# A hybrid decoder trunk: the places of the pooled parts on their way to DRAM, and the temporaries of the input sums

## The chip, the core and the metric

The kernel runs on one core of a Trainium2 chip. The core has five engines with instruction streams of their own: TensorE (PE) multiplies matrices out of SBUF into PSUM; VectorE (DVE) and ScalarE (ACT) do elementwise work; GpSimd (POOL) and SyncE (SP) here only issue transfers (DMAs). An engine takes its instructions in order and waits at one whose semaphores are not there yet. The metric is the device time in microseconds (us) of one execution; the median of three runs counts.

## The reference

One layer with two residual steps on x (512 tokens, 1024 channels, fp32). Cut to what matters:

```python
h = _rms(x, norm1_w) * (1 + sc1) + sh1
z, xbc, dt_raw, q, k, v, u, gates = split(h @ w_in)
y_ssd  = ssd(xbc, dt_raw, z) @ w_ssd_out
y_attn = dilated_attention(q, k, v) @ w_attn_out
y_pool = (_multi_scale_pool(u, w_pool_mix) * pool_scale) @ w_pool_out
g_ssd, g_attn, g_pool = split(sigmoid(gates))
x = x + g1 * ((g_ssd * y_ssd + g_attn * y_attn + g_pool * y_pool) @ w_out)
h = _rms(x, norm2_w) * (1 + sc2) + sh2
x = x + g2 * (square(relu(h @ w_ff1)) @ w_ff2)
```

The pooling takes the 1024 channels of u in four groups of 256. Each group gets the mean over its window (2, 4, 8 or 16 tokens) less u itself, and then a 256 x 256 matrix of its own:

```python
outs.append((csg - shifted) / count - ug[:, :, gi])      # group gi
pooled = stack(outs);  einsum('bsgi,gio->bsgo', pooled, w_pool_mix)
```

## The kernel before

**Tiles.** Activations lie with channels on the 128 partitions and 512 tokens along them, in SBUF tiles of 128 x 512. Such tiles live in 49 equal places. `blk(name)` takes the place that has been idle longest, `free` puts a place at the end of the list of idle ones; who takes a place waits until everything that read or wrote it has finished, a transfer to DRAM included. The eight PSUM banks are handed out by the same rule.

**Products.** Each fp32 product is made of three matmuls (`mm3`, L305 to L307): both factors are split into a high part (the value rounded to fp32r) and a low part (the rest), and high x low, high x high and low x high are added in PSUM. A weight pair (128 x 1024) is loaded by SP into `raw`, cast by ScalarE into `wh`, and its low part `wl` is made by VectorE (L288), or, in the stretch of this change (`st["adds"]`, `wsplit_add`), by ScalarE writing the negative of `wh` (L281) and POOL issuing an accumulating transfer of the weight onto it (L282).

**The stretch of the change.** After the attention's projection come, on TensorE, the products for u (`pool`), the gate of the SSD branch, `gate(GS, 0)`, with the four groups of the pooling's mixing put between its weight pairs, and the product with w_ssd_out, `project(a["w_ssd_out"], 8, 0, ...)`, whose first matmul in the profile is `psacc<-ynl,wh`. `project` needs four PSUM banks; two of them are those that the last mixing group leaves.

`pool_mix(gi)` does one mixing group: for each half m (128 channels) six matmuls into a bank `psmix`, then ScalarE writes the high part x, scaled, into SBUF (L1164), VectorE the low part y (L1165), the bank is freed, and POOL issues the transfers of both to DRAM (L1169). They are brought back much later as `poolh` and `pooll`. The SBUF places of x and y are the list `stage`: four of them, taken at the first group and used by all four groups, x and y of half m in `stage[2 * m : 2 * m + 2]`, so that each group writes where the group ahead of it is still being sent from. They are freed after the last group.

`input_sums(xh, xl)` makes sums of the eight input tiles that `seven_products` needs (a product of two-by-two blocks with seven block products instead of eight; its matmuls are L823). Four pieces, k = 0 to 3; each adds high and low part of tiles k and k + 4 into t1 and t2 (L765, L766: full width, 128 x 512), forms x and y in four half-width steps (L767 to L770), and splits x and y into `txh`, `txl`, `tyh`, `tyl` (a ScalarE cast L332 and a VectorE subtraction L333 each). Each piece takes four places for t1, t2, x and y and frees them at its end. It is used twice: during the gate and w_ssd_out's product (the pieces are spread between weight pairs, `side.extend(sums)`), for all gates after it, and in the MLP (all four pieces at once, ahead of `second(0)`).

**What sets the order.** The code is traced in the order it is written; pieces of side work are traced by `tick()` after each weight pair. A scheduler then sets the order of each engine's instructions by its own estimates of when operands and places are there, with preference for what stands in `tc.high_priority`. So another place for a tile, and with it another set of waits, also gives another order. `seven_products` sums its weights on VectorE with high priority (`wsum` and `rawl`, L805 to L808, from `rawl` and `raw` loaded by SP, L789 and L790); those of the gate that follows are made in this stretch already.

Of the kernel before, what the change touches and what calls it, by code (L numbers as in the profile page):

```python
# [11 lines left out]
F32R = mybir.dt.float32r  # L12
# [86 lines left out]
def kernel(ctx: ExitStack, tc: tile.TileContext, a: dict, out: bass.AP, dbg=None):  # L99
# [35 lines left out]
    def blk(name, dt=F32):  # L135
        return sb.take(name, dt)
# [620 lines left out]

    def input_sums(xh, xl):

        tq = []  # L760

        def piece(k):
            def go():
                t1, t2, x, y = (blk("tq") for _ in range(4))
                V.tensor_tensor(t1, xh[k].bitcast(F32), xl[k].bitcast(F32), ALU.add)  # L765
                V.tensor_tensor(t2, xh[k + 4].bitcast(F32), xl[k + 4].bitcast(F32), ALU.add)  # L766
                V.tensor_tensor(x[:, ta], t1[:, tb], t1[:, ta], ALU.subtract)  # L767
                V.tensor_tensor(x[:, tb], t2[:, tb], x[:, ta], ALU.subtract)
                V.tensor_tensor(y[:, ta], t2[:, tb], t1[:, tb], ALU.subtract)
                V.tensor_tensor(y[:, tb], t2[:, ta], x[:, tb], ALU.subtract)  # L770
                tq.append((split(x, "tx"), split(y, "ty")))
                free(t1, t2, x, y)

            return go

        return tq, [piece(k) for k in range(4)]
# [376 lines left out]
    def pool_mix(gi):  # L1153
        wh, wl = mixw[gi]
        if gi == 0:

            stage.extend(blk("pool", F32R) for _ in range(4))
        for m in range(2):
            ps = psm("mix")
            cs = slice(m * P, (m + 1) * P)  # L1160
            for k in range(2):
                mm3(ps, wh[:, k, cs], wl[:, k, cs], dh[2 * gi + k], dl[2 * gi + k], k == 0, k == 1)
            x, y = stage[2 * m : 2 * m + 2]
            S.activation(x, ps, AF.Copy, scale=vc("pool_scale", gi * 2 + m))  # L1164
            V.scalar_tensor_tensor(y, ps, vc("pool_scale", gi * 2 + m), x.bitcast(F32), ALU.mult, ALU.subtract)  # L1165
            free(ps)
            for t, l in ((x, ph_), (y, pl_)):
                l.append(dp.tile([P, T], F32, name=uid("pool")))
                nc.gpsimd.dma_start(l[-1], t.bitcast(F32))  # L1169
        if gi == 3:  # L1170
            free(*stage)
        free(*dh[2 * gi : 2 * gi + 2], *dl[2 * gi : 2 * gi + 2])
# [375 lines left out]
```

## Time and profile before

| | |
|---|---|
| median of 3 runs | 1096.71 us (1096.25 to 1097.31) |
| profiled execution | 1095.79 us, its span 1094.0 us |
| granted TensorE clock, mean | 0.998 |
| busy: TensorE, VectorE, ScalarE, POOL | 1083.0, 748.4, 548.2, 39.9 us |

A timeline row gives the start in the span, the duration, engine, line, operation, output and inputs, and in brackets how long the engine had been idle and what ended that. Starts one after another on an engine are closer than the durations, since instructions overlap. "DMA to landing" is the time from the issue of a transfer to its end. Names in the profile are without numbers: `pool<-psmix,vec` is a high part of the pooling, `pool<-psmix,vec,pool` a low part, `tq` are the sums' temporaries, `psacc` a bank of a product.

### The profile page before, as it was taken

The page shows a single profiled execution, that of the slowest core. Times are in us where ns is not written, and L with a number is a line of the kernel's source. Part 1 is how long each engine was busy: PE and PEld are TensorE (multiplying, and loading weights), DVE is VectorE, ACT ScalarE, POOL GpSimd, SP SyncE. Part 2 cuts the span into 40 slices and gives each one's busy share as a digit, 9 for nine tenths or more (in the row PEclk, how much of TensorE's full clock was granted, in tenths as well). Part 3 has the DMA queues.
Part 4 walks back from the last instruction along what each step waited for, and adds up shares of the span by engine and source line. Part 5 has one row for each costly group of instructions (what it writes and reads, how often), then busy time and mean ns, then how long its engine had stood idle before and what let it go on. Part 6 is the DMA issues. An engine that isn't in the chain of part 4 may idle for free.

```text
span 1094.0 us, 15636 instructions
## 1 busy us (share of the span) xinstructions
PE 1083.0 (99%) x6022; PEld 935.0 (85%) x6022; DVE 748.4 (68%) x1429; ACT 548.2 (50%) x889; POOL 39.9 (4%) x70
## 2 busy tenths in 40 slices
PE   8999999999999999999989999999999999999998
PEld 7878888888887888888869889899889989989987
DVE  7955746683677966667866657567697587687664
ACT  8965874543544943756455335354344334335330
POOL 0000000000000010001311100000000000000000
PEclk9999999999999999999999999999999999999999
DMA  9823253546554343247855543460214224233032
GB/s 342 305 97 91 68 158 120 191 154 203 182 174 146 105 142 101 78 121 189 242 179 181 146 135 116 138 228 1 84 52 155 74 80 136 63 111 136 20 116 77
DMA packets 50958, 148.71 MB, mean 136 GB/s; under 512 B 6066, under 2 KB 6834, under 8 KB 50884
## 3 DMA queue, kind: packets, MB, share of 16 engines
q1 hardware_dynamic: 43088, 126.08, 34.5%
q0 software_dynamic: 7072, 20.45, 7.6%
q10 hardware_dynamic: 724, 1.18, 0.3%
q8 instruction: 47, 0.77, 0.3%
q14 instruction: 27, 0.22, 0.1%
HBM read 141.37 MB, written 6.32 MB: 135 GB/s over the span
## 4 chain that ended last, share of the span: by engine, by line
PE 95%; DVE 2%; DMA 1%; ACT 1%; issue 0%; SPq 0%; POOL 0%; DVEq 0%; ACTq 0%
PE psacc L305 22%; PE psacc L306 22%; PE psacc L307 22%; PE psacc L823 17%; PE psacc L545 4%; PE psS L624 1%; PE psy L1084 1%; DMA pool<-pool 1%; PE pso L740 1%; PE psyo L1092 1%; PE pso L738 1%; DMA xT<-in_x_dram 0%; PE psqT L603 0%; PE pskT L608 0%; PE psst L1043 0%; PE pspT L721 0%
## 5 line engine op out<-in xcount | busy, mean ns | idle before, releaser
L288 DVE TENSOR_TENSOR wl<-raw,wh 128x1024 fp32r<-128x1024 f32 x116 | 141.6, 1221 | 128.6 <-ACT wh L288 120.7
L288 ACT CAST wh<-raw 128x1024 fp32r<-128x1024 f32 x116 | 121.6, 1049 | 188.6 <-PE psacc L306 108.3
L305 PE MATMUL psacc<-hl,wh 128*128 128x512 f32 x320 | 128.8, 403 | 0.2 <-ACT pT L722 0.2
L307 PE MATMUL psacc<-hh,wl 128*128 128x512 f32 x320 | 124.7, 390 | 0.0
L306 PE MATMUL psacc<-hh,wh 128*128 128x512 f32 x320 | 124.6, 389 | 0.0
L306 PE MATMUL psacc<-ah,wh 128*128 128x512 f32 (+1 forms) x260 | 100.4, 386 | 0.0
L305 PE MATMUL psacc<-al,wh 128*128 128x512 f32 (+1 forms) x260 | 100.4, 386 | 0.0
L307 PE MATMUL psacc<-ah,wl 128*128 128x512 f32 (+1 forms) x260 | 100.3, 386 | 0.0
L305 PE MATMUL psacc<-wl,rh 128*128 128x512 f32 x192 | 77.4, 403 | 0.0
L307 PE MATMUL psacc<-wh,rl 128*128 128x512 f32 x192 | 75.2, 392 | 0.0
L306 PE MATMUL psacc<-wh,rh 128*128 128x512 f32 x192 | 75.1, 391 | 0.0
L305 PEld LDWEIGHTS psacc<-hl,wh 128*128 128x128 f32 x320 | 60.1, 188 | 13.5 <-issue 1.2
L306 PEld LDWEIGHTS psacc<-hh,wh 128*128 128x128 f32 x320 | 60.2, 188 | 13.3 <-issue 1.4
L307 PEld LDWEIGHTS psacc<-hh,wl 128*128 128x128 f32 x320 | 60.0, 188 | 12.8
L1467 DVE SCALAR_TENSOR_TENSOR xr<-psacc,modv,xr 128x512 f32<-128x512 f32 (+1 forms) x65 | 44.7, 738 | 18.7 <-PE psacc L307 18.7
L799 DVE TENSOR_TENSOR wl<-rawl,wh 128x512 fp32r<-128x512 f32 (+1 forms) x36 | 33.6, 953 | 34.5 <-ACT wh L798 34.4
L307 PEld LDWEIGHTS psacc<-ah,wl 128*128 128x128 f32 x260 | 48.8, 188 | 9.8
L305 PEld LDWEIGHTS psacc<-al,wh 128*128 128x128 f32 x260 | 48.9, 188 | 9.7
L306 PEld LDWEIGHTS psacc<-ah,wh 128*128 128x128 f32 x260 | 48.9, 188 | 9.7
L798 ACT CAST wh<-wsum 128x1024 fp32r<-128x1024 f32 x18 | 19.0, 1053 | 70.9 <-PE psacc L306 69.0
L798 ACT CAST wh<-rawl 128x512 fp32r<-128x512 f32 (+1 forms) x36 | 29.1, 833 | 48.7 <-PE psacc L306 28.3
L305 PEld LDWEIGHTS psacc<-wl,rh 128*128 128x128 f32 x192 | 36.1, 188 | 7.7 <-ACT qT L604 0.5
(426 smaller groups left out, 2781.1 us busy)
## 6 DMA issues: line engine op xcount, KB each, us to landing
raw<-in_w_in_dram SPq DMA_DIRECT2D x74, 512.0 KB, 3.6
raw<-in_w_ff_dram SPq DMA_DIRECT2D x52, 512.0 KB, 3.7
wa<-in_w_ada_dram SPq DMA_DIRECT2D x64, 256.0 KB, 3.5
wada<-in_w_ada_dram SPq DMA_DIRECT2D x14, 512.0 KB, 7.9
rawl<-in_w_ff_dram SPq DMA_DIRECT2D x12, 512.0 KB, 3.5
wst<-in_w_in_dram SPq DMA_DIRECT2D x16, 256.0 KB, 7.8
M<-prow POOLq DMA_DIRECT2D x16, 256.0 KB, 3.7
wl<-in_w_in_dram POOLq DMA_DIRECT2D x8, 512.0 KB, 5.7
```

Of the source, the lines that this page charges most:

```text
L288: edges[:] = S.copy(wh, raw), V.tensor_tensor(wl, raw, wh.bitcast(F32), ALU.subtract)
L305: mm(ps, lhsT=wh, rhs=xl, start=first, stop=False)
L306: mm(ps, lhsT=wh, rhs=xh, start=False, stop=False)
L307: mm(ps, lhsT=wl, rhs=xh, start=False, stop=last)
L545: mm(ps[j], lhsT=t[:, j, :], rhs=w, start=first, stop=last)
L624: mm(so[b], lhsT=qT[:, b * P : (b + 1) * P], rhs=kT[:, (b + 1) * P - n : (b + 1) * P], start=True, stop=True)
L738: mm(od, lhsT=vs[kb][:, hs], rhs=pT[b // 2][:, cs : cs + P], start=(b == 0), stop=False, skip_group_check=True)
L740: mm(ov[:, b, :], lhsT=vs[b][:, hs], rhs=pT[0][:, b * P : (b + 1) * P], start=False, stop=(gi == 2 and b == 3), skip_group_check=True)
L798: S.copy(h, x)
L799: V.tensor_tensor(l, x, h.bitcast(F32), ALU.subtract)
L823: mm(o, lhsT=x[:, cs], rhs=y, start=first and k == 0 and j == 0 and n == 0, stop=k == 3 and n == 2, skip_group_check=True)
L1467: V.scalar_tensor_tensor(xT[d][:, ts], p[:, : ts.stop - ts.start], modv[:, 3, d : d + 1], xT[d][:, ts], ALU.mult, ALU.add)
```

## The change

Two edits. `pool_mix` takes eight places at the first group instead of four, and groups 0 and 2 use the first four, groups 1 and 3 the other four. `input_sums` takes the four temporaries once, at the first piece, all pieces use them, and they are freed after the last.

```diff
     def input_sums(xh, xl):
-        tq = []
+        tq, tmp = [], []
         def piece(k):
             def go():
-                t1, t2, x, y = (blk("tq") for _ in range(4))
+                if k == 0:
+                    tmp.extend(blk("tq") for _ in range(4))
+                t1, t2, x, y = tmp
...
                 tq.append((split(x, "tx"), split(y, "ty")))
-                free(t1, t2, x, y)
+                if k == 3:
+                    free(*tmp)
...
         if gi == 0:
-            stage.extend(blk("pool", F32R) for _ in range(4))
+            stage.extend(blk("pool", F32R) for _ in range(8))
...
-            x, y = stage[2 * m : 2 * m + 2]
+            x, y = stage[4 * (gi % 2) + 2 * m : 4 * (gi % 2) + 2 * m + 2]
```

The number of instructions on each engine is the same. The lines behind the first edit move down by 3: L1165 is L1168 in the changed kernel, L805 is L808, and the sums L765 to L770 are L767 to L772. On POOL and SP the order is the same; on TensorE one matmul of w_ssd_out's product stands later. VectorE and ScalarE differ around the mixing groups and around the MLP's pieces. The rows that follow have the names with their numbers; the last number of a name counts all tiles.

VectorE around group 1 of the mixing (psmix_1034 and psmix_1037 before, psmix_1038 and psmix_1041 now, are the banks of its two halves; wsum is the first weight sum of the gate to come). Before:

```order
L1165 SCALAR_TENSOR_TENSOR pool_1019_4898<-psmix_1034_4965,vec_1_79,pool_1018_4897 128x512
L765 TENSOR_TENSOR tq_1080_5197<-hh1_247,hl1_255 128x512
L333 TENSOR_TENSOR pdl_1010_4859<-win_1008_4853,pdh_1009_4858 128x512
L765 TENSOR_TENSOR tq_1069_5148<-hh0_246,hl0_254 128x512
L767 TENSOR_TENSOR tq_1071_5150<-tq_1069_5148 128x256
L1165 SCALAR_TENSOR_TENSOR pool_1021_4900<-psmix_1037_4978,vec_1_79,pool_1020_4899 128x512
L805 TENSOR_TENSOR wsum_1116_5335<-rawl_1110_5321,raw_1111_5322 128x2x256
L768 TENSOR_TENSOR tq_1071_5150<-tq_1070_5149,tq_1071_5150 128x256
```

Now, in the same place (the wsum is row 687 of VectorE):

```order
L1168 SCALAR_TENSOR_TENSOR pool_1023_4902<-psmix_1038_4969,vec_1_79,pool_1022_4901 128x512
L1168 SCALAR_TENSOR_TENSOR pool_1025_4904<-psmix_1041_4982,vec_1_79,pool_1024_4903 128x512
L333 TENSOR_TENSOR pdl_1010_4859<-win_1008_4853,pdh_1009_4858 128x512
L768 TENSOR_TENSOR tq_1074_5153<-hh4_250,hl4_258 128x512
L769 TENSOR_TENSOR tq_1075_5154<-tq_1073_5152 128x256
L771 TENSOR_TENSOR tq_1076_5155<-tq_1074_5153,tq_1073_5152 128x256
L770 TENSOR_TENSOR tq_1075_5154<-tq_1074_5153,tq_1075_5154 128x256
L808 TENSOR_TENSOR wsum_1108_5327<-rawl_1102_5313,raw_1103_5314 128x2x256
```

The second low part of the group (pool_1021 before, pool_1025 now) moved ahead of the sums, right behind the first; behind it three half-width sums of the first piece stand ahead of the weight sum.

VectorE around group 3, the last (banks psmix_1052 and psmix_1055 before, psmix_1056 and psmix_1059 now). Before:

```order
L768 TENSOR_TENSOR tq_1104_5297<-tq_1103_5296,tq_1104_5297 128x256
L766 TENSOR_TENSOR tq_1092_5247<-hh6_252,hl6_260 128x512
L1165 SCALAR_TENSOR_TENSOR pool_1019_4898<-psmix_1052_5079,vec_1_79,pool_1018_4897 128x512
L1165 SCALAR_TENSOR_TENSOR pool_1021_4900<-psmix_1055_5092,vec_1_79,pool_1020_4899 128x512
L805 TENSOR_TENSOR wsum_1117_5340<-rawl_1112_5325,raw_1113_5326 128x2x256
L806 TENSOR_TENSOR rawl_1112_5325<-rawl_1112_5325 128x2x256
L807 TENSOR_TENSOR wsum_1117_5340<-wsum_1117_5340,rawl_1112_5325 128x2x256
L333 TENSOR_TENSOR txl_1085_5208<-tq_1082_5199,txh_1084_5207 128x512
```

Now, from row 701:

```order
L772 TENSOR_TENSOR tq_1076_5155<-tq_1074_5153,tq_1075_5154 128x256
L333 TENSOR_TENSOR txl_1085_5208<-tq_1075_5154,txh_1084_5207 128x512
L768 TENSOR_TENSOR tq_1074_5153<-hh6_252,hl6_260 128x512
L769 TENSOR_TENSOR tq_1075_5154<-tq_1073_5152 128x256
L770 TENSOR_TENSOR tq_1075_5154<-tq_1074_5153,tq_1075_5154 128x256
L1168 SCALAR_TENSOR_TENSOR pool_1023_4902<-psmix_1056_5083,vec_1_79,pool_1022_4901 128x512
L1168 SCALAR_TENSOR_TENSOR pool_1025_4904<-psmix_1059_5096,vec_1_79,pool_1024_4903 128x512
L333 TENSOR_TENSOR tyl_1087_5212<-tq_1076_5155,tyh_1086_5211 128x512
```

The subtraction txl of the second piece, which stood behind the last group's two low parts, stands ahead of them now; it is row 702, and its place is one that group 2 was sent from.

ScalarE behind group 3, up to the last weight pair of the product (wh_1100 and wl_1101 before, wh_1096 and wl_1097 now). Before:

```order
L1164 ACTIVATE pool_1020_4899<-psmix_1055_5092,vec_1_79 128x512
L332 CAST tyh_1086_5211<-tq_1083_5200 128x512
L280 CAST wh_1100_5266<-raw_1099_5264 128x1024
L281 ACTIVATE wl_1101_5267<-wh_1100_5266 128x1024
L332 CAST txh_1106_5305<-tq_1104_5297 128x512
```

Now:

```order
L1167 ACTIVATE pool_1024_4903<-psmix_1059_5096,vec_1_79 128x512
L332 CAST tyh_1086_5211<-tq_1076_5155 128x512
L332 CAST txh_1091_5252<-tq_1075_5154 128x512
L280 CAST wh_1096_5262<-raw_1095_5260 128x1024
L332 CAST tyh_1093_5256<-tq_1076_5155 128x512
L281 ACTIVATE wl_1097_5263<-wh_1096_5262 128x1024
```

Two casts of the third piece (txh_1091, tyh_1093) moved ahead of the negative that makes the last weight's low part, one of them between the weight's two steps.

## The prediction

> **What bounds the kernel now.** I read the page's head first.
>
> ```profile
> span 1094.0 us, 15636 instructions
> ...
> PE 1083.0 (99%) x6022; PEld 935.0 (85%) x6022; DVE 748.4 (68%) x1429; ACT 548.2 (50%) x889; POOL 39.9 (4%) x70
> ```
>
> TensorE is busy 99% of the span, so an edit on other engines can shorten the program only where TensorE stands still or runs at a lower clock. Its list of waits says where that is (total, times, longest):
>
> ```profile
> PE psacc L305 <- DVE pool L1165: 4.1, 1, 4.1
> ```
>
> The list is sorted; the others are smaller. TensorE's timeline shows it in place (start, us, instruction, idle before it and releaser), the windows the granted clock (the column behind POOL busy):
>
> ```profile
> 547.71 0.39 PE L305 MATMUL psacc<-ynl,wh 128*128 128x512 f32 x1
> ...
> 550.21 0.39 PE L307 MATMUL psacc<-ynh,wl 128*128 128x512 f32 x1
> 554.67 0.79 PE L305 MATMUL psacc<-ynl,wh 128*128 128x512 f32 x1 [4.08 <-DVE pool L1165]
> 555.26 0.63 PE L306 MATMUL psacc<-ynh,wh 128*128 128x512 f32 x1
> ...
> 558.23 0.40 PE L305 MATMUL psacc<-ynl,wh 128*128 128x512 f32 x1
> ```
>
> ```profile
> 554.00:556.00 2.00, 1.33 (x3) 1.14 (x4) 1.41 (x3) 0.41 (x1) 1.64 (x4) 0.57 1.10 328
> 556.00:558.00 2.00, 2.00 (x6) 1.53 (x6) 1.85 (x3) 0.00 (x0) 0.51 (x1) 0.58 1.01 231
> 558.00:560.00 2.00, 2.00 (x10) 1.64 (x9) 0.00 (x0) 0.00 (x0) 0.00 (x0) 1.00 1.00 399
> ```
>
> From 547.71 to 550.21 are 11 steps of 0.227 us. The next matmul, the 13th of the first half of w_ssd_out's product, was due at 550.44 and starts at 554.67: 4.23 late. From there to 558.23 nine steps take 3.56 instead of 2.04, at a clock of 0.57 to 0.58, and then it is 1.00: 1.52 more. The stall and its tail cost **5.75 us**, and nothing else within reach of the change costs TensorE anything.
>
> I follow the releaser back. The matmul needs a PSUM bank that pool_mix's last group must leave:
>
> ```profile
> 532.23 0.69 ACT L1164 ACTIVATE pool<-psmix,vec 128x512 fp32r<-128x512 f32 x1 [0.86 <-DMA pool<-pool]
> ...
> 536.80 1.05 ACT L280 CAST wh<-raw 128x1024 fp32r<-128x1024 f32 x1 [3.38 <-PE psacc L306]
> ...
> 541.90 1.06 ACT L281 ACTIVATE wl<-wh 128x1024 fp32r<-128x1024 f32 x1
> ...
> 547.37 0.62 ACT L332 CAST txh<-tq 128x512 fp32r<-128x512 f32 x1 [2.76 <-DVE tq L768]
> 548.01 1.28 ACT L344 ACT_TABLE_LOAD   x1
> ...
> 553.13 1.29 ACT L1164 ACTIVATE pool<-psmix,vec 128x512 fp32r<-128x512 f32 x2
> 560.68 0.62 ACT L332 CAST tyh<-tq 128x512 fp32r<-128x512 f32 x1 [6.27 <-DMA pool<-pool]
> ```
>
> ```profile
> 539.65 0.75 DVE L1165 SCALAR_TENSOR_TENSOR pool<-psmix,vec,pool 128x512 fp32r<-128x512 f32 x1 [4.32 <-DMA pool<-pool]
> 540.32 0.68 DVE L805 TENSOR_TENSOR wsum<-rawl,raw 128x512 f32<-128x512 f32 x1
> 540.92 0.42 DVE L768 TENSOR_TENSOR tq<-tq,tq 128x256 f32<-128x256 f32 x1
> 541.25 0.69 DVE L806 TENSOR_TENSOR rawl<-rawl 128x512 f32<-128x512 f32 x1
> ...
> 546.92 0.42 DVE L768 TENSOR_TENSOR tq<-tq,tq 128x256 f32<-128x256 f32 x1
> ...
> 553.87 1.41 DVE L1165 SCALAR_TENSOR_TENSOR pool<-psmix,vec,pool 128x512 fp32r<-128x512 f32 x2 [3.60 <-ACT pool L1164]
> ```
>
> ```profile
> 531.66 2.49 POOL L1169 DMA_DIRECT2D pool<-pool  x4
> ...
> 543.25 0.90 POOL L282 DMA_DIRECT2D wl<-in_w_ssd_out_dram  x1 [2.01 <-ACT wl L281]
> ...
> 552.58 0.90 POOL L282 DMA_DIRECT2D wl<-in_w_ssd_out_dram  x1 [5.61 <-ACT wl L281]
> ...
> 563.65 0.90 POOL L282 DMA_DIRECT2D wl<-in_w_ssd_out_dram  x1 [7.14 <-ACT wl L281]
> ```
>
> Read backwards: TensorE at 554.67 is 0.80 behind VectorE's L1165 at 553.87, that is 0.74 behind ScalarE's L1164 at 553.13, that closes an unbroken run (cast, table load, sigmoids, one weight) since ScalarE's cast txh at 547.37, that is 0.45 behind VectorE's L768 at 546.92. VectorE runs unbroken back to 539.65, where it waited 4.32 us for a transfer: group 1's second low part takes the place from which group 0's still goes to DRAM (issued in the run of four from 531.66, landed 8.0 us later). That wait starts the chain.
>
> **Part 1, eight places.** Group 1 no longer takes group 0's places, so VectorE's 4.32 and ScalarE's 0.86 go. What is late next on VectorE is row 687, the weight sum, which needs a transfer of SP's:
>
> ```profile
> 531.36 0.33 SPq L789 DMA_DIRECT2D rawl<-in_w_in_dram  x1
> ```
>
> ```profile
> DMA to landing us min/median/max: 5.0/5.0/5.0
> ```
>
> The sum can start at 531.36 + 5.0 = 536.36; VectorE, through at 539.65 - 4.32 = 535.33 before, has 0.73 more ahead of it now (a second L1168 and two half-width sums for one full-width sum, by the steps below): 536.06, so the transfer ends last. The four rows from 539.65 give the steps from start to start: 0.67 out of PSUM, 0.60 at full width, 0.33 at half width. From 536.36 stand, in the new order, L808 wsum (536.36), L772 tq (536.96), L809 (537.29), L810 (537.89), two full-width sums (538.49, 539.09), txl (539.69), two L1168 of group 2 (540.29, 540.96), tyl (541.63), three half-width sums (542.23, 542.56, 542.89). The last takes 0.42 and releases ScalarE's txh at 543.31; with the 0.03 that the row of 547.37 stood behind its sum's end, 543.34. That is **4.03 earlier**. ScalarE's work ahead of it is done by then: the weight wl of 541.90 stood behind a txh whose sum now comes ahead of VectorE's wait, so it follows its wh of 536.80 at 537.85, 4.05 earlier; group 2's two L1164 (PSUM ready by 539.6) and tyh end by 541.6.
>
> From there the run of ScalarE is the same work in the same order; group 3's mixing matmuls end by 547.71, ahead of ScalarE's L1164 at 549.10. So L1168 starts at 549.84 and TensorE at 550.64. In the new order TensorE wants that bank one matmul earlier, at 550.21, so 0.43 stays. The second bank follows 0.67 later and is wanted 0.78 later: nothing. The transfer that landed at 539.65 is still waited for, now by group 2's second low part, which comes at 540.96: 1.3 us of cover; if that went, each us would cost one.
>
> Does the clock drop after 0.43? No row has such a gap; the nearest is
>
> ```profile
> 252.71 0.50 PE L305 MATMUL psacc<-hl,wh 128*128 128x512 f32 x1 [0.18 <-ACT pT L722]
> ```
>
> ```profile
> 252.00:254.00 2.00, 1.81 (x11) 1.41 (x10) 2.00 (x4) 2.00 (x5) 0.00 (x0) 1.00 0.81 252
> ```
>
> a gap of 0.18 with the clock at 1.00 and one matmul 0.11 longer. The bounds are 0 (that row) and 1.52 (a gap of 4.08, the rows above); 0.43 is far nearer to 0.18, so I take 0.1, and the residual is **0.53**. [...]
>
> Price of the extra traffic: group 1's last part is sent from about 534 instead of 540.7, while the weight sum's source is in flight. A part is 128 x 512 x 4 = 262 KB; at the rate of a full window,
>
> ```profile
> 548.00:550.00 2.00, 2.00 (x11) 1.65 (x10) 1.97 (x5) 1.98 (x3) 0.00 (x0) 1.00 1.01 408
> ```
>
> that is 0.64 us if it went wholly ahead. It is issued 2.7 us behind that source, so I take 0; the other end is 0.64.
>
> **Part 2, shared temporaries.** The number of sums is the same. Three pieces now write temporaries that the piece ahead must have been read out of, so pieces run one after another. In the table of sums only one piece lies on the chain, counted above. Two other ends of it go by landings, of the pooled parts' transfers and of POOL's eight weight accumulations here (least, median, longest):
>
> ```profile
> DMA to landing us min/median/max: 2.6/4.4/8.0
> ```
>
> ```profile
> DMA to landing us min/median/max: 5.1/5.8/7.8
> ```
>
> First, txl of row 702 takes a stage place just freed and now stands ahead of group 3's two L1168. It needs group 2's first transfer, issued at 539.8 (the weight's accumulation comes 4.0 earlier than 543.25, with ScalarE's weight, and POOL's transfer 0.57 behind). Landings of such transfers are 2.6 to 8.0 us, so 542.4 to 547.8; txl, one full-width and two half-width sums follow, 1.86, so VectorE is free by 549.7 at the latest, ahead of 549.84: 0 at both ends, with 0.1 to spare at the long one.
>
> Second, the last accumulated weight. Its ScalarE step now stands behind tyh, which waits for one of group 3's transfers (before, the tyh of 560.68 did, 8.1 behind the weight of 552.58). Now 552.58 - 4.03 + 8.1 = 556.65; tyh 0.55, the weight 1.06 and 0.25 to POOL give 558.5; with landings of 5.1, 5.8 and 7.8 it is there at 563.6, 564.3 or 566.3. TensorE wants it 22 matmuls ahead of this row:
>
> ```profile
> 575.27 0.28 PE L823 MATMUL psacc<-hl,wh 128*128 128x256 f32 x1
> ```
>
> 575.27 - 22 x 0.227 - 5.22 = 565.06. So the cost is 0 to 1.3; I take 0, by the median. The sums that this row starts to use are done by about 561 in the chain above, 9 us ahead: nothing.
>
> The waits that sharing adds fall on VectorE: a piece's sums overwrite what ScalarE's cast and VectorE's own subtraction of the piece ahead must have read. Those subtractions now stand ahead of them in VectorE's order, so what is queued behind such a wait is only the next piece, and once the two cases above. In the MLP four pieces stand in a row:
>
> ```profile
> 784.18 1.23 DVE L288 TENSOR_TENSOR wl<-raw,wh 128x1024 fp32r<-128x1024 f32 x1 [2.86 <-ACT wh L288]
> 788.80 0.69 DVE L805 TENSOR_TENSOR wsum<-rawl,raw 128x512 f32<-128x512 f32 x1 [3.39 <-DMA raw<-in_w_ff_dram]
> ...
> 812.59 0.68 DVE L333 TENSOR_TENSOR tyl<-tq,tyh 128x512 fp32r<-128x512 f32 x1
> ```
>
> Before, the last piece is spread to 812.59. Now all of it stands ahead of the sum of 788.80, and between the weight ahead of 784.18 and that weight stand 3.7 us instead of 1.0 (three full-width, four half-width steps and one subtraction instead of three half-width ones): 2.7 more into an idle time of 2.86. I take 0. The other end, if two casts of ScalarE (0.6 each) are waited for there, is 1.2 of a late weight.
>
> **Sum.** 5.75 - 0.53 = **5.2 us** gained. The profiled execution took 1095.79 (its span is 1094.0), 0.92 under the median of 1096.71; it would be 1090.6, and the median 1096.71 - 5.2 = **1091.5**.
>
> **Rivals.** *A smaller gain.* The residual grows: the last weight late (1.3), the source of the weight sum late (0.64), the clock halved again (1.52). One or two of them together leave 2.4 to 4.6, 1092.1 to 1094.3, at the middle 1093.2. The clock alone gives 1091.5 + 1.5 = 1093.0, and has 0.05 of this case's 0.18. For it: three steps have little cover. Against: each takes the unfavourable end of a range.
>
> *A wait that takes the place of the one removed.* VectorE's weight sum waits for its source from 536.36; were that to land as late after its issue as the part that was waited for (8.0 instead of 5.0, 539.4), the chain would be 1.0 earlier instead of 4.0, the clock would halve as before, and the time is 1095.7; from 539.0 to 540.4 it is 1095.3 to 1096.7: no change. For it: the same 16 engines move both. [...] Against: 3 us is near five parts at 0.64, and only one more is in flight.
>
> *Slower.* Row 702's txl stands ahead of group 3's L1168 and needs a transfer of group 2; before, it stood behind. If that lands later than 552.0 (12.2 after its issue), L1168 starts later than 553.87, TensorE later than 554.67, and each us costs one; at 14 us it is 1.8 late, 1098.5. For it: it is a new wait on the only path that matters. Against: the longest landing in the trace is 8.0.
>
> **How the numbers follow.** Main case 0.64 (1090.5 to 1092.1: a residual of 0 to 1.1, and at the lower end half a us for the spread of the runs, 1096.25 to 1097.31), a smaller gain 0.18, no change 0.12, slower 0.06. The range takes the first two: 1090.5 to 1094.3, 0.82. About 0.2%, 2.2 us, is what a measurement can tell from no change: faster 0.82, same 0.12, slower 0.06.
>
> **What would show it.** Right: TensorE's wait on L1168 is below 1 us and the clock near 550 to 558 stays at 1.00; VectorE's L1168 of group 1 waits for no transfer; VectorE's longest wait there is L808 for rawl, to about 536.4; ScalarE's txh near 543.3. Wrong: TensorE still waits 2 us or more there, or a new wait on wl shows near 565, or VectorE's txl waits for pool beyond 549.8, or TensorE waits appear in the MLP after 788.

## The result, and the profile after

| | before | after |
|---|---|---|
| median (least to greatest) | 1096.92 us (1096.25 to 1097.31) | 1090.81 us (1090.45 to 1092.66) |
| ratio, 95% interval | | 0.9949 (0.9934 to 0.9964) |
| profiled execution, its span | 1095.79, 1094.0 us | 1090.45, 1088.7 us |

The changed kernel is faster: by the ratio of the runs 5.6 us, with an interval of 4.0 to 7.2; the medians differ by 6.1. The forecast was 5.2 us and 1091.5. The page's head after:

```profile
span 1088.7 us, 15639 instructions
...
PE 1081.3 (99%) x6022; PEld 934.0 (86%) x6022; DVE 748.1 (69%) x1429; ACT 547.6 (50%) x889; POOL 39.8 (4%) x70
```

The busy times are those of before within 2 us; only the time in which TensorE stood still, or ran at half clock, is shorter. Its list of waits (total, times, longest) has the same entry with another number, below a larger one at the program's start:

```profile
PE pssx L423 <- DVE sq L432: 1.3, 1, 1.3
PE pswarm L416 <- DVE ones L385: 1.1, 1, 1.1
PE psacc L305 <- DVE pool L1168: 0.8, 1, 0.8
```

TensorE's timeline, in place (the first row is the first matmul of w_ssd_out's product; the last, L826, is the first matmul of the seven-product blocks that follow it):

```profile
547.03 0.39 PE L305 MATMUL psacc<-ynl,wh 128*128 128x512 f32 x1
...
549.29 0.39 PE L306 MATMUL psacc<-ynh,wh 128*128 128x512 f32 x1
550.50 0.50 PE L305 MATMUL psacc<-ynl,wh 128*128 128x512 f32 x1 [0.82 <-DVE pool L1168]
550.85 0.40 PE L306 MATMUL psacc<-ynh,wh 128*128 128x512 f32 x1
...
569.95 0.28 PE L826 MATMUL psacc<-hl,wh 128*128 128x256 f32 x1
```

The windows there (busy times of the five engines, then granted clock, DMA share, GB/s):

```profile
550.00:552.00 2.00, 1.50 (x6) 1.21 (x7) 1.71 (x3) 1.27 (x3) 1.77 (x4) 1.00 1.05 268
552.00:554.00 2.00, 2.00 (x10) 1.64 (x9) 1.98 (x4) 0.40 (x1) 0.35 (x1) 1.00 0.99 215
```

The matmul that waits was due 0.23 behind 549.29 and starts at 550.50: 0.98 late. The one behind it comes 0.35 later instead of 0.23: 0.12 more. The clock stays at 1.00. So the stall and its tail cost 1.10 us instead of 5.75, and 4.65 are gained.

One measure serves for all kernels below: **the stretch** from the product's first matmul to the first of L826. It holds 96 matmuls; at 0.227 us each it would be 21.8 us. Before it is 575.27 - 547.71 = 27.56, after 569.95 - 547.03 = 22.92: 4.64 less. From there to the end of the span it is 518.73 before and 518.75 after: the rest of the program, the MLP with it, gained and lost nothing. Ahead of it the program came to 547.03 instead of 547.71, 0.68 earlier. TensorE waits for nothing of the change there, and the 0.68 arose at the program's start, far ahead of the mixing groups: the first matmul of L545 starts at 16.73 before and at 16.05 after, and from there to 547 the distance stays the same within 0.05. In the eleven executions of the experiments the product's start lies between 547.04 and 549.11, once at 553.18; that 0.68 is chance. The profiled execution is 5.34 us shorter: 4.64, 0.68 and 0.02 of rounding.

VectorE, from group 1's low parts to group 3's:

```profile
531.31 1.41 DVE L1168 SCALAR_TENSOR_TENSOR pool<-psmix,vec,pool 128x512 fp32r<-128x512 f32 x2
...
536.21 0.69 DVE L808 TENSOR_TENSOR wsum<-rawl,raw 128x512 f32<-128x512 f32 x1 [1.28 <-DMA rawl<-in_w_in_dram]
...
546.74 0.69 DVE L333 TENSOR_TENSOR txl<-tq,txh 128x512 fp32r<-128x512 f32 x1 [2.63 <-ACT wh L280]
...
548.40 0.43 DVE L770 TENSOR_TENSOR tq<-tq,tq 128x256 f32<-128x256 f32 x1
549.70 1.41 DVE L1168 SCALAR_TENSOR_TENSOR pool<-psmix,vec,pool 128x512 fp32r<-128x512 f32 x2 [0.87 <-ACT pool L1167]
```

Group 1's two low parts run as a pair, with no bracket: the wait of 4.32 us on a transfer is gone. In its place stands the weight sum, which waits 1.28 us for SP's transfer, to 536.21. The 2.63 us ahead of txl at 546.74 are longer, but VectorE stands idle once more behind them, so they are off the chain. ScalarE, and the transfer that VectorE waited for, with its time to landing:

```profile
543.21 0.62 ACT L332 CAST txh<-tq 128x512 fp32r<-128x512 f32 x1 [2.94 <-DVE tq L770]
...
548.96 1.28 ACT L1167 ACTIVATE pool<-psmix,vec 128x512 fp32r<-128x512 f32 x2
...
557.26 0.62 ACT L332 CAST tyh<-tq 128x512 fp32r<-128x512 f32 x1 [2.60 <-DMA pool<-pool]
557.79 1.06 ACT L281 ACTIVATE wl<-wh 128x1024 fp32r<-128x1024 f32 x1
```

```profile
530.67 0.33 SPq L792 DMA_DIRECT2D rawl<-in_w_in_dram  x1
```

```profile
DMA to landing us min/median/max: 5.4/5.4/5.4
```

The chain is now: the transfer of 530.67 lands 5.4 us later, the weight sum at 536.21, ScalarE's txh at 543.21, its L1167 at 548.96, VectorE's L1168 at 549.70, TensorE at 550.50.

### The profile page after: what moved, and what is told of

It is laid out like the page before. It is cut to its first block, busy times and chain, and to the rows that moved or that the text cites. A ratio compares the mean times of both kernels' runs of the same rounds, so it can differ in the third digit from the quotient of the medians.

```text
span 1088.7 us, 15639 instructions
## 1 busy us (share of the span) xinstructions
PE 1081.3 (99%) x6022; PEld 934.0 (86%) x6022; DVE 748.1 (69%) x1429; ACT 547.6 (50%) x889; POOL 39.8 (4%) x70
## 4 chain that ended last, share of the span: by engine, by line
PE 96%; DVE 2%; DMA 1%; ACT 1%; issue 1%; SPq 0%; DVEq 0%; ACTq 0%
PE psacc L305 22%; PE psacc L307 22%; PE psacc L306 22%; PE psacc L826 17%; PE psacc L545 4%; PE psS L624 1%; PE psy L1087 1%; PE pso L740 1%; PE psyo L1095 1%; PE pso L738 1%; DMA rawl<-in_w_in_dram 1%; PE psqT L603 0%; PE pskT L608 0%; PE psst L1046 0%; PE pspT L721 0%
```

## The experiments

The theory on record has these parts: the eight places take away a wait of VectorE; what is left is set by the landing of the weight sum's source; the order that comes with the shared temporaries costs nothing; and a short gap leaves the clock alone. Against it stand the prediction's rivals and one more, that the shared temporaries do the work: the sum's source lands later by the extra traffic; the early txl is a wait on the path; the last weight comes late. The table gives all profiled executions (stretch, TensorE's waits in it, the lowest granted clock of a 2 us window behind the wait) and the times of each kernel with its ratio to the kernel before on the same chip.

| kernel | stretch | bank wait, last weight's wait | lowest clock | median us | ratio (95%) |
|---|---|---|---|---|---|
| before | 27.56 | 4.08, - | 0.57 | 1096.92 | |
| after | 22.92 | 0.82, - | 1.00 | 1090.81 | 0.9949 (0.9934 to 0.9964) |
| after_again | 23.09 | 1.04, - | 1.00 | 1091.48 | 0.9949 (0.9937 to 0.9961) |
| after_third | 23.42 | 1.37, - | 1.00 | 1091.07 | 0.9957 (0.9943 to 0.9971) |
| e1_eight | 25.72 | 2.04, - | 0.50 | 1093.87 | 0.9968 (0.9956 to 0.998) |
| e2_shared | 28.95 | 4.34, - | 0.50 | 1097.0 | 1.0 (0.9992 to 1.0009) |
| e6_twice | 24.37 | 2.33, - | 1.00 | 1093.83 | 0.9969 (0.9957 to 0.9982) |
| e7_five | 25.56 | 1.83, - | 0.50 | 1093.45 | 0.9965 (0.9952 to 0.9978) |
| e8_late | 23.30 | -, 1.24 | 1.00 | 1091.84 | 0.995 (0.9933 to 0.9966) |
| e9_before_late | 27.75 | 2.01, 1.76 | 0.55 | 1096.38 | 0.9991 (0.9979 to 1.0003) |
| e10_late_swap | 22.89 | -, 0.79 | 1.00 | 1090.85 | 0.9951 (0.9934 to 0.9967) |
| e15_late3_shift | 22.29 | -, 0.2 | 1.00 | 1090.39 | 0.9945 (0.9932 to 0.9958) |
| e16_late4_shift | 21.78 | -, - | 1.00 | 1089.98 | 0.9943 (0.9931 to 0.9955) |

From the end of the stretch to the end of the span it is 518.69 to 518.79 us in every one of them, so the stretch holds all that any of these edits did.

### The changed kernel twice again

No edit; each ran on the same chip as other kernels of the table (after_again with e1_eight, e2_shared and e10_late_swap, after_third with e15_late3_shift and e16_late4_shift).

> The changed kernel again, beside the experiments. Theory T (the gain is the wait for the PSUM bank of the last mixing group and the halved clock behind it): TensorE's wait for L1168 is 0.8 us as in the first profile, the clock stays at 1.00, and the time is 1090.8, 5.2 to 6.1 under the kernel before. Rival C (the clock halves behind a short wait in some executions): the single times fall in two heaps 1.5 us apart, near 1090.5 and 1092. Rival S (part of the 6 us is chance at the program's start): the first matmul of w_ssd_out's product stands anywhere from 547.0 to 547.7, as it did in the two profiles.

> The changed kernel a third time, for the comparison with the two that follow. Theory T: TensorE waits 0.8 to 1.0 us for L1168, the stretch from the first matmul of w_ssd_out's product to the first seven-product matmul takes 22.9 to 23.1 us, and the time is 1091.

VectorE's weight sum, and the landing of its source, in the one and in the other:

```profile
536.89 0.69 DVE L808 TENSOR_TENSOR wsum<-rawl,raw 128x512 f32<-128x512 f32 x1 [1.51 <-DMA rawl<-in_w_in_dram]
```

```profile
DMA to landing us min/median/max: 5.7/5.7/5.7
```

```profile
537.25 0.69 DVE L808 TENSOR_TENSOR wsum<-rawl,raw 128x512 f32<-128x512 f32 x1 [1.82 <-DMA rawl<-in_w_in_dram]
```

```profile
DMA to landing us min/median/max: 6.0/6.0/6.0
```

Against the product's first matmul (547.03, 547.50 and 547.53) the sum starts at -10.82, -10.61 and -10.28, and TensorE waits 0.82, 1.04 and 1.37. What the sum is later, 0.21 and 0.54, TensorE waits longer, 0.22 and 0.55. So the residual varies with this one landing, us for us: 5.4, 5.7 and 6.0. The third execution's wait and stretch, 1.37 and 23.42, lie outside what was expected for it. Rival S holds: the product starts anywhere from 547.03 to 547.53. Rival C is not settled: in these three profiles the clock stays at 1.00, but of the sixteen timed executions of this kernel three show a mean of 0.998 (1092.66, 1092.04 and 1095.18 us), as much as the kernel before loses in its profile, and where in those executions it was lost is not on record.

### Each half alone: e1_eight and e2_shared

e1_eight is the kernel before with the eight places only:

```diff
-            stage.extend(blk("pool", F32R) for _ in range(4))
+            stage.extend(blk("pool", F32R) for _ in range(8))
-            x, y = stage[2 * m : 2 * m + 2]
+            x, y = stage[4 * (gi % 2) + 2 * m : 4 * (gi % 2) + 2 * m + 2]
```

> Eight places, each piece with four temporaries of its own as before. Theory T: group 1's wait is gone here too, but two of the second piece's temporaries take stage places that group 2 is still sent from, so VectorE waits for landings at about 546.7 to 547.9 and has eight steps (3.9 us) more to do ahead of group 3's low parts: these start at about 550.5 instead of 549.7, TensorE's wait is about 2.0 us, and the time is 1091.8: 1.0 over the changed kernel, 5 under the one before. Rival (the sharing does nothing, the places do all): the time is that of the changed kernel, 1090.8. Rival (the sharing does most): near 1096.

VectorE late in the stretch, and the windows behind TensorE's wait:

```profile
547.56 0.69 DVE L766 TENSOR_TENSOR tq<-hh,hl 128x512 f32<-128x512 f32 x1 [3.15 <-DMA pool<-pool]
...
551.84 1.40 DVE L1165 SCALAR_TENSOR_TENSOR pool<-psmix,vec,pool 128x512 fp32r<-128x512 f32 x2
```

```profile
552.00:554.00 2.00, 1.36 (x4) 1.13 (x5) 1.67 (x3) 0.00 (x0) 1.12 (x3) 0.76 0.94 201
554.00:556.00 2.00, 2.00 (x6) 1.51 (x6) 1.56 (x3) 0.00 (x0) 0.48 (x1) 0.50 1.03 324
```

The wait came as the theory had it: the places alone take 2.0 us off 4.08. Then a sum of the next piece waits 3.15 us for a temporary's place from which a pooled part is still being sent. The changed kernel's txl waits for such a transfer too, and against the product's first matmul no less long (546.74 - 547.03 there, 547.56 - 548.17 here); what differs is the work behind it, nine rows of VectorE ahead of group 3's L1165 instead of four. The clock halves on top, so the stretch is 2.8 us longer than in the changed kernel, 1.2 of it by the wait, and the time is 2 us over what was expected. The seven runs show the clock too: three with a mean of 0.999 or 1.000 took 1091.4 to 1092.8, four with less 1093.9 to 1095.6.

e2_shared is the changed kernel with four places, so the shared temporaries only:

```diff
-            stage.extend(blk("pool", F32R) for _ in range(8))
+            stage.extend(blk("pool", F32R) for _ in range(4))
-            x, y = stage[4 * (gi % 2) + 2 * m : 4 * (gi % 2) + 2 * m + 2]
+            x, y = stage[2 * m : 2 * m + 2]
```

> Shared temporaries, four places as before. Theory T: VectorE still waits about 4.3 us for the transfer of group 0's last part, to 539.6; of the sums behind it as many stand ahead of ScalarE's txh as before (547.3 instead of 547.4), so TensorE waits 4 us with the halved clock behind, and the time is that of the kernel before within 0.4 us, 1096.7. Rival (the sharing does most): 1091 to 1093.

VectorE at group 1's second low part, and the landing of the weight sum's source there:

```profile
539.73 0.75 DVE L1168 SCALAR_TENSOR_TENSOR pool<-psmix,vec,pool 128x512 fp32r<-128x512 f32 x1 [3.59 <-DMA pool<-pool]
```

```profile
DMA to landing us min/median/max: 5.6/5.6/5.6
```

The wait of before is there and the time is that of before, 1.0 (0.9992 to 1.0009). The shared temporaries are worth nothing without the places; with them, 1093.87 - 1091.48 = 2.4 us on the same chip, more than half of it through the clock (of the 2.8 between the stretches 1.2 are wait). The source lands 5.6 us after its issue here, with group 1's parts sent as late as before: a landing over 5.0 needs no extra traffic.

### Extra traffic and the early txl: e6_twice

The changed kernel, with each of group 1's four parts sent a second time to a scratch tensor that nobody reads:

```diff
+                if gi == 1:
+                    nc.gpsimd.dma_start(dp.tile([P, T], F32, name=uid("twice")), t.bitcast(F32))
```

> The changed kernel, with group 1's four parts sent to DRAM a second time (work added: 1 MB into places that nothing reads). Theory T with the prediction's slower rival as its price: four more transfers of about 0.6 us lie ahead of group 2's first one, which lands at about 549 instead of 546.7; VectorE's txl waits for it, and group 3's low parts start at about 551.0 instead of 549.7: TensorE's wait is 2.1 instead of 0.8, the time 1092.1. Rival (landings are covered by ScalarE's chain): TensorE's wait stays at 0.8, 1090.8. Rival N (the source of the weight sum shares the engines): rawl lands a us or more later and the whole chain moves by as much on top.

VectorE, and the window behind TensorE's wait:

```profile
549.22 0.69 DVE L333 TENSOR_TENSOR txl<-tq,txh 128x512 fp32r<-128x512 f32 x1 [5.26 <-DMA pool<-pool]
...
551.23 1.40 DVE L1168 SCALAR_TENSOR_TENSOR pool<-psmix,vec,pool 128x512 fp32r<-128x512 f32 x2
```

```profile
552.00:554.00 2.00, 1.97 (x9) 1.61 (x10) 1.23 (x2) 0.00 (x0) 1.60 (x3) 1.00 1.05 240
```

This is the mechanism of the slower rival made to happen: the txl ahead of group 3's low parts waits for a transfer, to 549.22 instead of 546.74. Of these 2.5 us VectorE's idle time of 0.87 covers a part, and 1.5 reach TensorE, whose wait grows from 0.82 to 2.33: beyond the cover, one for one. That transfer, group 2's first, was issued later, at 541.40 instead of 539.13; from its issue to txl it is 7.8 us, against 7.6 in the changed kernel. POOL issued eight transfers from 530.42 to 534.18, three of the extra ones among them, and the next at 539.49, after 4.44 us of idle time that its row puts down to a sum of VectorE (L768); what held POOL up there is not shown. The source of the weight sum landed after 5.3 us, no later than without the extra traffic (three of the four extra transfers were under way by then): the other rival isn't seen. In this profiled execution the clock stayed at 1.00 after a gap of 2.33; its time was 1091.89, near the 1092.1 expected, but seven of the nine runs took 1093.7 to 1095.7, all with a mean clock of 0.997 or 0.998.

### Five places: e7_five

```diff
-            stage.extend(blk("pool", F32R) for _ in range(8))
+            stage.extend(blk("pool", F32R) for _ in range(5))
-            x, y = stage[4 * (gi % 2) + 2 * m : 4 * (gi % 2) + 2 * m + 2]
+            x, y = stage[2 * m], stage[4 if m and gi % 2 else 2 * m + 1]
```

> Shared temporaries as in the changed kernel, but only one place more than before, five: group 1's second low part (the one that waited 4.3 us) and group 3's have a place of their own. Theory T: VectorE's wait in group 1 goes as with eight places, but group 2 then waits for group 1's transfers: ScalarE's second part of group 2 for a landing at about 543 us, so ScalarE's txh starts 1.7 us later than with eight places; TensorE's wait is about 2.5 us, the time 1092.5. Rival (only the one wait mattered): as the changed kernel, 1090.8. Rival (the wait of group 2 takes all back): 1096.

ScalarE in group 2's mixing, and the window behind TensorE's wait:

```profile
541.96 0.69 ACT L1167 ACTIVATE pool<-psmix,vec 128x512 fp32r<-128x512 f32 x1 [1.45 <-DMA pool<-pool]
...
544.47 0.62 ACT L332 CAST txh<-tq 128x512 fp32r<-128x512 f32 x1 [1.82 <-DVE tq L770]
```

```profile
554.00:556.00 2.00, 2.00 (x6) 1.52 (x6) 1.48 (x3) 0.00 (x0) 0.00 (x0) 0.50 0.99 320
```

One more place, given to the one low part that VectorE waited for, takes the wait from 4.08 to 1.83, less than was expected to remain. The waits move on to group 2, which meets group 1's transfers, and txh starts 2.81 ahead of the product's first matmul (547.28) instead of 3.82. The clock halves: the stretch is 2.6 longer than in the changed kernel for 1.0 more of wait, and the time is 1.0 over what was expected.

### TensorE asks for the banks later: e8_late and e9_before_late

With `late=4` the matmuls of the product's first two weight pairs (each holds two steps of k, so four) go to the two banks that are there first, and the other two banks' matmuls of those steps come behind them. The sums in each bank are the same, in the same order.

```diff
-        ps = [acc() for _ in range(4)]
+        ps, held = [acc() for _ in range(4)], []
...
-            for j in range(4):
+            held.append((k, wh, wl))
+            turns = [(held[-1], j) for j in range(2 if k < late else 4)]
+            if k == late - 1:
+                turns += [(x, j) for x in held for j in (2, 3)]
+            for (n, h, l), j in turns:
...
-    project(a["w_ssd_out"], 8, 0, yh, yl, sg)
+    project(a["w_ssd_out"], 8, 0, yh, yl, sg, late=4)
```

e8_late puts this into the changed kernel, e9_before_late into the kernel before.

> The changed kernel with the first of the two edits of the run with both: the bank of the last mixing group is wanted 24 matmuls after the product's start instead of 11, the eight places are freed first, as in the changed kernel. Theory T: no wait for the bank, 1.1 gained; but ScalarE's tyh, which waits for group 3's transfer until about 557.3, now stands ahead of both steps of the last weight, whose low part lands at about 565.5 and is wanted at 563.8: TensorE waits 1.7 for wl, and the time is 1091.4, 0.6 over the changed kernel. Rival (the weight is in time): 1089.7.

> The kernel before (four places, temporaries of each piece) with only the later want of the bank, 24 matmuls after the product's start. Theory T: the bank is free at 554.7 as before and wanted at 553.2, so the wait is 1.5 instead of 4.1; TensorE is then 4.2 us earlier at the last weight, which lands at 569.3 as before and is wanted at 566.1: it waits 3.2 there. The time is 1095.7, 1 under the kernel before, and up to 1.5 more if the clock halves. Rival (the weight is in time): 1092.7. Rival (the bank was not the cause): 1096.9.

ScalarE in e8_late, and the wait on TensorE's timeline:

```profile
557.72 0.62 ACT L336 CAST tyh<-tq 128x512 fp32r<-128x512 f32 x1 [6.06 <-DMA pool<-pool]
558.25 1.05 ACT L280 CAST wh<-raw 128x1024 fp32r<-128x1024 f32 x1
559.32 1.06 ACT L281 ACTIVATE wl<-wh 128x1024 fp32r<-128x1024 f32 x1
```

```profile
566.26 0.50 PE L307 MATMUL psacc<-ynh,wl 128*128 128x512 f32 x1 [1.24 <-DMA wl<-in_w_ssd_out_dram]
```

The bank wait is gone, and the last weight is late instead: the new order puts tyh, which waits for a transfer of group 3, ahead of both steps of that weight on ScalarE (in the changed kernel ahead of the second only, 557.79). Against the product's first matmul the weight's second step is 0.5 us later than in the changed kernel, and with no wait for the bank TensorE wants the weight 1.1 us earlier; there were 0.6 to spare. That is the mechanism of the prediction's late weight, at a somewhat smaller price than expected. In e9_before_late both waits stand, of a bank and of the last weight:

```profile
PE psacc L305 <- DVE pool L1169: 2.0, 1, 2.0
PE psacc L307 <- DMA wl<-in_w_ssd_out_dram: 1.8, 1, 1.8
```

Its time is 0.9991 (0.9979 to 1.0003) of the kernel before, against 0.9949 for the change, and the last weight cost about half of what was expected: with only the order of TensorE's product edited, what the bank gives is lost to the weight and to the clock (0.55). Asking later, by itself, doesn't do it here.

### Whose places the pieces take: e10_late_swap

e8_late, and the idle places of the mixing's inputs go on the list ahead of those of the pooled parts:

```diff
+        free(*dh[2 * gi : 2 * gi + 2], *dl[2 * gi : 2 * gi + 2])
...
-        free(*dh[2 * gi : 2 * gi + 2], *dl[2 * gi : 2 * gi + 2])
```

> The changed kernel, with two more edits: in the first half of w_ssd_out's product the first two weight pairs go into two banks first and into the other two after, so that TensorE wants the bank of the last mixing group 24 matmuls after the product's start instead of 11; and the mixing's inputs are freed ahead of the eight places, so that the last weight's low part no longer stands behind a cast that waits for group 3's transfers. Theory T: the bank is free at about 550.5 and wanted at 552.5, so no wait is left; the last weight is there about 1 us early; the time is 1.1 us under the changed kernel, 1089.7, and if rival C holds, the heap at 1092 is gone too. Rival (another wait takes its place): TensorE waits for wl near 563 to 566, and the time is 1090.8 or more.

ScalarE there:

```profile
562.45 0.62 ACT L336 CAST tyh<-tq 128x512 fp32r<-128x512 f32 x1 [4.69 <-DVE tq L776]
562.98 1.05 ACT L280 CAST wh<-raw 128x1024 fp32r<-128x1024 f32 x1
```

This missed: a wait of 0.79 on the last weight is left. The cast no longer waits for a transfer of the pooled parts, but it still stands ahead of the weight, and waits for VectorE's sums instead (this execution ran about 5 us later from its start: the product's first matmul is at 553.18, and the run took 1096.57 where four of the six took 1090.2 to 1091.4). Against the product's first matmul the weight's second step stands where the changed kernel has it (564.05 - 553.18 = 10.87, there 557.79 - 547.03 = 10.76); with no wait for the bank TensorE wants it 1.1 us earlier. So as long as the cast stands ahead of the weight, whatever the cast itself waits for, the gain at the bank is mostly paid at the weight.

### The casts behind the weight: e15_late3_shift and e16_late4_shift

The changed kernel with `late=3` and `late=4` (the first three and the first four steps of k), and the last two pieces of the sums one weight pair later:

```diff
-    side.extend(sums)
+    side.extend(sums[:2])
+    rest(1)
+    side.extend(sums[2:])
```

> The changed kernel with the bank of the last mixing group wanted 18 matmuls after the product's start instead of 11, and the third and fourth pieces of sums traced one weight pair later, so that both steps of the last weight stand ahead of the casts that wait for group 3's transfers. Theory T: the bank is free 3.5 us after the product's start and wanted after 4.1, the last weight lands about 2 us ahead of its want: no wait is left, the stretch takes 96 x 0.227 = 21.8 us, and the time is 1.1 to 1.3 us under the changed kernel beside it: 1089.7. Rival (a wait moves behind the stretch, to the sums or weights of the seven products): the stretch is 21.8 but what follows it is longer than 518.7.

> As the run with 18 matmuls, with 24. Theory T: the same time, 1089.7; the last weight is cast only when the first pair's place is free, 36 matmuls after the product's start, and lands about 0.9 us ahead of its want. Rival (it lands late): a wait for wl of up to 1 us, and 1090.7.

ScalarE and TensorE in e16_late4_shift:

```profile
556.91 1.06 ACT L281 ACTIVATE wl<-wh 128x1024 fp32r<-128x1024 f32 x1
557.88 0.60 ACT L336 CAST txh<-tq 128x512 fp32r<-128x512 f32 x1
```

```profile
547.69 0.39 PE L305 MATMUL psacc<-ynl,wh 128*128 128x512 f32 x1
...
569.47 0.28 PE L830 MATMUL psacc<-hl,wh 128*128 128x256 f32 x1
```

Now the weight's second step stands ahead of the casts. Nothing of the bank or the weight is waited for, and the stretch is 21.78 us: 96 matmuls at 0.227 and nothing else. TensorE takes the last weight at 564.48, 6.2 us behind the issue of its transfer at 558.27, and does not wait; that is within the landings of these transfers before, 5.1 to 7.8. With `late=3`, where it was to land 2 us ahead, it came 0.2 late: the matmul that needs it starts at 566.26, 8.1 behind the end of ScalarE's negative (558.18). With the slower first matmuls behind that and at the bank 0.5 us is left. So the 1.1 us that the change left are a bank's lateness and nothing more, and they can be had. On the same chip e16_late4_shift took 1089.98 and the changed kernel 1091.07; the intervals of their ratios to before overlap (0.9931 to 0.9955 and 0.9943 to 0.9971), so the times alone don't tell them apart, the stretches do (21.78 against 22.92, 23.09 and 23.42).

## Why the prediction was right, and where it was short

**The wait that goes: right.** Group 1's low parts wait for no transfer, VectorE's longest wait around that group is L808 for `rawl`, TensorE's wait is 0.82 and the clock is 1.00. e1_eight and e2_shared show that the places, not the sharing, take it away. In the two later executions TensorE's wait is 1.04 and 1.37, past the 1 us that the prediction gave as its sign.

**The sum's start at 531.36 + 5.0: too early, the one term that was mis-sized.** The duration came from one landing of before. After, it was 5.4 (and 5.7 and 6.0 in the two later executions), and the sum started about 0.1 behind the landing, a step that the prediction put at nothing. Against the product's first matmul the sum was to start at 536.36 - 547.71 = -11.35 and started at -10.82, 0.53 later; txh was forecast at -4.37 and came at -3.82, L1168 at 2.13 and 2.67, TensorE at 2.93 and 3.47. So every link behind it kept the length that the rows of before gave, to 0.02. The residual became 1.10 instead of 0.53, the gain in the stretch 4.64 instead of 5.2. The prediction's main case allowed a residual of 1.1 at most; the later executions passed it, with 1.3 and 1.6 (23.09 and 23.42 less 21.8). The total was nearer than its terms: in the profiled executions 0.68 of the program's start, by chance, made up the difference. In the medians, 6.1 apart, a second thing adds. The profiled execution of before, with a mean clock of 0.998, is a cheap one: beside after_again seven of the 18 runs of before show 0.998 and took 1096.2 on average, ten show 0.997 and took 1097.0. So the 1.52 for the clock comes from the cheaper kind; where the others lose more is not on record, but e2_shared's profile, at 0.997, loses it behind this same wait.

**Price of the extra traffic, taken at 0 with 0.64 as the other end: not settled, and smaller than the spread.** The landing took 5.0 us in before and 5.6 in e2_shared, in which group 1's last part is sent as late as before. In six executions in which that part is sent early it took 4.8 to 6.2, 5.5 on average: 5.4, 5.7 and 6.0 in the changed kernel, 5.1 in e7_five, 4.8 in e8_late, 6.2 in e10_late_swap. With three extra transfers under way (e6_twice) it took 5.3. Whether one more part in flight adds anything can't be told from that. What the prediction lacked was the spread of this one landing, from 4.8 to 6.2.

**txl of row 702, cost 0: right, with 0.87 us to spare.** Its bracket names a ScalarE step long done; the other releaser is group 2's transfer:

```profile
539.13 0.89 POOL L1172 DMA_DIRECT2D pool<-pool  x1
```

```profile
DMA to landing us min/median/max: 7.5/7.5/7.5
```

539.13 + 7.5 is 546.6, and txl starts at 546.74. It comes near the long end of the range of before (8.0), and VectorE still stands idle for 0.87 us ahead of L1168 at 549.70. That range itself did not hold: the longest landing of a pooled part after is 10.1 us, of a part of group 1 that nothing on the chain waits for. e6_twice shows the price once that cover is used up.

**The last weight, cost 0: right, with luck in it.** Its transfer and landing:

```profile
559.14 0.90 POOL L282 DMA_DIRECT2D wl<-in_w_ssd_out_dram  x1 [6.80 <-ACT wl L281]
```

```profile
DMA to landing us min/median/max: 5.2/5.2/5.2
```

It is there at 564.3 and wanted 22 matmuls ahead of 569.95, at 565.0: 0.6 to spare. Against the product's first matmul its transfer was issued 1.3 us later than forecast (559.14 - 547.03 = 12.11 instead of 558.5 - 547.71 = 10.8), since tyh waited that much longer for its own; a landing at the short end of the range (5.2 of 5.1 to 7.8) and a want 0.6 later made up for it. With the 5.8 that the prediction took the weight would have come just in time. In e8_late, where the cast stands ahead of both steps and TensorE does not wait for the bank, 1.24 is paid.

**The MLP, cost 0: right.** 518.73 and 518.75 from the seven-product blocks to the end.

**The clock, 0.1 taken: right for this gap, with less room than the text had.** After gaps of 0.82, 1.04 and 1.37 (the three profiled executions of the changed kernel) the profiles show 1.00 and one matmul 0.11 longer. After 1.83 (e7_five), 2.01 (e9_before_late) and 2.04 (e1_eight) the clock halves, and what lies in the stretch beyond the wait and 21.8 us is 1.9 us (e1_eight: 25.72 - 21.8 - 2.04; e7_five the same) against 0.3 in the changed kernel. In e6_twice a gap of 2.33 did not halve it, nor did the second gap of e9_before_late, 1.76 (steps of 0.23 us behind it); so the length of the gap alone doesn't say, and what else decides is not shown. The prediction had rows at 0.18 and 4.08 only.

How long the half lasted is in the traces. Before, by windows of 0.2 us, the clock is 0.50 from 554.27 to 557.68, 3.41 us. The windows of 2 us give 3.40 us in e1_eight (0.76, 0.50 and 0.89 from 552 to 558) and in e7_five (0.82, 0.50 and 0.83 there), 3.44 in e9_before_late (0.59 and 0.55 from 556 to 560), and in e2_shared at least 6.72, up to 560 (0.82 and three times 0.50 from 552 on). So its price, as an estimate from these numbers, is half of what is left of that time when TensorE starts again: (557.68 - 554.67) / 2 = 1.5 before, where the rows gave 1.52, and 1.7 in e1_eight, where the whole of it lies behind the gap.

**The rivals.** That the sum's source lands at 539.4 or later: in the nine profiled executions whose landing is on record it came 4.8 to 6.2 after its issue, never 8.0. That txl makes it slower: the mechanism is real, and the landing of 7.5 us left 0.87 us of cover. That the gain is smaller: its source of the weight sum did come later, by 0.4 to 0.5 us, and in the profiled execution neither the last weight nor the clock was added to it.

## What to carry to other kernels

When a wait on a buffer's release is removed, ask what is late next on the same engine, and if that is a single transfer, put the spread of its landings into the estimate, not one of them: here most of the miss, and the whole variation of the residual over three executions, was that landing. A pool that hands out places in the order in which they were freed passes the wait on to whoever takes the place, so more places for one user can be lost again at the next one; count all users. And where TensorE waited for 1.8 us or more, the clock halved in five of six profiled executions (0.50 to 0.57 in a window of 2 us), and 1.7 to 2.8 us lay in the stretch beyond the waits and 21.8 us (before 1.7, e1_eight and e7_five 1.9, e9_before_late 2.2, e2_shared 2.8; e6_twice, at 1.00, 0.2), so that shortening a gap from 2.04 us (e1_eight) to 1.04 (after_again) was worth 2.6 here.

## What the runs showed of the hardware beyond that

The half clock can outlast its gap: in e1_eight 3.40 us of it follow a gap of 2.04, and e2_shared, after 4.34 us, ran at

```profile
554.00:556.00 2.00, 1.32 (x3) 1.13 (x4) 1.88 (x3) 1.45 (x3) 1.63 (x4) 0.50 1.05 320
556.00:558.00 2.00, 2.00 (x6) 1.52 (x6) 1.59 (x4) 0.00 (x0) 0.53 (x1) 0.50 1.01 225
558.00:560.00 2.00, 2.00 (x7) 1.52 (x6) 1.58 (x4) 0.22 (x1) 0.00 (x0) 0.50 1.02 406
```

so its stretch is 28.95 - 21.8 - 4.34 = 2.8 us longer than wait and work, where before it was 1.7. The wait was longer by 0.26, the cost beyond it by 1.1, and the half lasted at least 6.72 us instead of 3.41. At the program's start the clock halves in some executions: e15_late3_shift, with a wait of 1.0 us there, ran at

```profile
10.00:12.00 2.00, 2.00 (x11) 2.00 (x11) 1.79 (x4) 1.94 (x3) 0.00 (x0) 0.50 1.10 367
```

and reached the product at 549.11, while e16_late4_shift, with a wait of 1.9 us at the same place, kept 1.00 and reached it at 547.69. In the execution of e10_late_swap that ran 5 us late the clock was 0.50 for 10.2 us between 10 and 22 (windows of 0.64, four of 0.50 and 0.80). No edit touches that place, so differences of 1 to 2 us between single executions, and once of 5, can come from there alone; the stretch is the better measure.
